# RWKV-7 and FFN step on one core: the end of the RWKV stage issued step by step between the first products of the first FFN

## The chip, the cores and the metric

One NeuronCore of a Trainium2 chip runs the whole kernel in one launch. The metric is the time of one execution on the device in microseconds (us). TensorE (PE) multiplies, VectorE (DVE) and ScalarE (ACT) do the elementwise work and empty PSUM, GpSimd (POOL) does a small share, and SyncE (SP) issues most of the DMA transfers; some are issued from ACT.

## The reference

The kernel computes one inference step of a two-layer decoder on 1024 prompt tokens and 64 sample tokens (8 requests of 8 tokens), 1088 tokens of width 1024 in all. Layer 0 mixes by a conformer convolution (512 channels) and by RWKV-7 (512 channels, 8 heads of 64); layer 1 mixes by pooling. After each mixing there is a SwiGLU FFN with a hidden width of 2816, and after each of the four sublayers a layer norm of the residual sum:

```
proj = x @ w_in
a_out, c_new = conformer_conv(proj[..., :1024], conv_prev, ...)
b_out, sh_new, s_new = rwkv_mix(proj[..., 1024:], shift_prev, wkv_prev, ...)   # o gets group norm, a bonus and a gate
mix = concat([a_out, b_out]) @ w_out
x = layer_norm(ALPHA * x + mix)
x = layer_norm(ALPHA * x + (silu(x @ wg) * (x @ wu)) @ wd)
```

rwkv_mix runs a recurrence over the tokens with one 64 x 64 state per head; the prompt is one sequence, the sample requests are eight short ones with states of their own.

## The kernel before

Tokens are cut into nine tiles: tiles 0 to 7 are 128 prompt tokens each, tile 8 the 64 sample tokens. Names in the program carry the tile's number; the trace leaves it out (`wo`, `xt`, `xo`, `bt_t`).

**Stages.** The in-projection, the convolution and the preparation of the recurrence (chunks, inverses of small triangular blocks on POOL) take the first part. A boundary follows in which the convolution halves of the out-projection (`wo<-hl_woA,ahl`) run while POOL inverts the last blocks. Then come eight RWKV loops (`chain`), one for each prompt tile, about 25 us each. Beside loop i the program issues filler work from a queue (`fq`): the preparation of the next tile, the group norm of the last (`gn_out`, tiles `gst_t`, `gmv_t`, `on_t`, then the transposes `pgn_t`, the gate `pg_t` and the gated output `bt_t`), the RWKV half of the out-projection of an older tile (`tail`, which is `wout`: 24 matmuls `wo<-hl_woB,bhl`, where `bhl` is `bt_t` split into two parts), and the transposes of a finished tile into the layout that the FFN reads (`xt`: 8 transposes of `y`, the scaling on ACT into `xo`, the store to `xtd` in DRAM).

**The end of the RWKV stage.** Behind loop 7 stand the sample unit (`chain_sample`: for each of four head pairs p the steps s0, products `sar` of the old state with mask `sm` and reduction `rS` on DVE; s1 and s2, products `spc`; s3, products `spo` and `sps` with mask `suv` and sums `Osb` and `ss`), the projections of tiles 6, 7 and 8, and the transposes of tiles 5 and 6. Only then the pools of the stage are closed and those of the FFN opened.

**FFN, first layer.** `early_x` loads the transposed activations of tokens 0 to 543 (`xe`, 4 loads of 544 KB) and splits them into the operands b11 and b21 (`b`). Stage 1a makes, for 11 pairs of blocks and for gate and up, one product of the upper left block of weights in two halves, which this text calls P1 (with b11) and P2 (with b21): 24 matmuls each, 44 halves in all. Two PSUM buffers of one tag hold a product (one for each 272 tokens), the tags taken in turn from `("mm", "o", "ch")`. After P1 ACT copies it out (`c`), after P2 ACT applies Silu (gate, `sg<-pa_g`) or DVE multiplies (up, `sg<-sg,pa_u`). P2 of a product stands behind P1 of the next. Weights are loaded (`raw_e`, 512 KB for a product) and split into `op_a` on ACT and DVE. `tick` issues one step of a second queue (`side`) about every 2 us of products: the transposes of tiles 7 and 8, then `late_x`, which loads all activations again (`xl`) and makes the operands t1 to t4 and b22 for stage 1b. Stage 1b begins with four sums of weight blocks on DVE (`s`, L1151) and their splits.

**Order.** On PE the order is the program's from loop 0 on. On the other engines a scheduler sets it at build time. PSUM has four tags (mm, o, ch, tp) of two buffers each.

The lines the change touches are in `phase2`, `chain_sample`, `gn_out`, `load_unit`, `early_x`, `load_w1`, `stage1a` and `build`.

Of the kernel before, what the change touches and what calls it, by code (L numbers as in the profile page):

```python
# [61 lines left out]
class Prog:  # L62
# [77 lines left out]
    def xt(self, l, i, y, pool, tag):  # L140
# [5 lines left out]
        def step(q):  # L146
            if q == 0:
                nc.scalar.dma_start(out=self.yd[l][i][:n], in_=y[:n])
# [36 lines left out]
    CAUTO = 8  # L185
# [7 lines left out]
    def consts(self, es, e1):  # L193
        tc, nc, I = self.tc, self.nc, self.I
        pool = lambda name, bufs=1, **kw: es.enter_context(tc.tile_pool(name=name, bufs=bufs, **kw))
        self.pp = pool("psum", 2, space=PSUM)
# [8 lines left out]
        self.c1d = [[self.dr.tile([128, TH], F32, name=f"c1d{l}_{x}") for x in range(NF)] for l in range(2)]  # L205
        self.hd = [[self.dr.tile([128, TOK], F32, name=f"hd{l}_{f}") for f in range(NF)] for l in range(2)]
# [12 lines left out]
    def phase1(self):  # L219
# [13 lines left out]
        pool = lambda name, bufs=1, **kw: es.enter_context(tc.tile_pool(name=name, bufs=bufs, side="right", **kw))  # L233
# [157 lines left out]
    def conv_a(self, i):  # L391
# [44 lines left out]
    def wout(self, i, get, w, alpha, after=None):  # L436
# [26 lines left out]
    def convs(self, wA):  # L463

        slots = []
        for x in range(11):
# [3 lines left out]
            if x >= 2:  # L470
                out += self.wout(x - 2, lambda j=x - 2: self.chl.pop(j), wA, ALPHA)
# [3 lines left out]
        return slots  # L475

# [191 lines left out]
    def load_unit(self, i):  # L668

        nc, up = self.nc, self.up  # L670
        u = type("Unit", (), {})()
        u.i, u.samp, u.nm = i, i == 8, f"t{i}"
# [7 lines left out]
        u.TT = up.tile([128, G, 64], F32, tag="TT", name=f"TT_{nm}")  # L680
# [8 lines left out]
        u.A21 = up.tile([128, G, 32], F32, tag="A21", name=f"A21_{nm}")  # L689
        u.ATm = [up.tile([128, G, 128], F32, tag=f"ATm{hd}", name=f"ATm{hd}_{nm}") for hd in range(2)]  # L690
# [5 lines left out]
        u.AR = up.tile([128, G, 2, 64], F32, tag="AR", name=f"AR_{nm}")  # L696
        u.BK = up.tile([128, G, 2, 64], F32, tag="BKh", name=f"BKh_{nm}")
        for t, d in ((u.AR, self.ard), (u.BK, self.bkd)):
            nc.sync.dma_start(out=t.rearrange("q (p c) s l -> q p (c s l)", p=4), in_=d[:, :, cs].rearrange("p q c s l -> q p (c s l)"))
        v = up.tile([128, 4, n], F32, tag="v", name=f"v_{nm}")  # L700
        u.bv = up.tile([128, 4, n], F32, tag="bv", name=f"bv_{nm}")
# [851 lines left out]
```

## Time and profile before

| | us |
|---|---|
| median of 3 runs (lowest, highest) | 2352.29 (2350.52, 2353.86) |
| the profiled execution | 2353.67 |
| its span | 2351.9 |
| PE busy | 2191.6 (93%) |
| DVE busy | 1558.9 (66%) |
| ACT busy | 910.3 (39%) |
| POOL busy | 449.3 (19%) |

The profile is one execution of the program with its instructions in time. Times in it count from the span's start. The profiled execution lies 1.38 us over the median. The granted clock (PEclk) is TensorE's clock as a share of full speed, averaged over a stretch.

### The profile page before, as it was taken

To read this page: it belongs to the slowest core of one execution; us is meant where nothing else is said; L and a number is where in the kernel's file an instruction comes from. 1 tells how busy PE (TensorE), PEld (TensorE's weight loads), DVE (VectorE), ACT (ScalarE), POOL (GpSimd) and SP (SyncE) were. 2 spreads that over 40 slices of the span, in tenths; PEclk is the share of its full clock that TensorE was granted. 3 is DMA by queue.
4 is the path that set the end of the run, shared out by engine and by line. 5 is a ranking of instruction groups with operands and counts; after the bars stand their busy time and mean duration, and the time that the engine had idled before them with its cause. 6 is when DMAs were issued, how large, how long until landed. Compare 5 with 4: busy or idle time off the path is not lost.

```text
span 2351.9 us, 39322 instructions
## 1 busy us (share of the span) xinstructions
PE 2191.6 (93%) x15026; PEld 1971.6 (84%) x15026; DVE 1558.9 (66%) x2859; ACT 910.3 (39%) x2041; POOL 449.3 (19%) x551
## 2 busy tenths in 40 slices
PE   8898898869896899999999999989999999999998
PEld 7887787657664799999997787879999999977886
DVE  6987698734457535777767657455477777667565
ACT  3243244445642543333333434343443333334332
POOL 3588866563111000000000101000000000000010
PEclk9999899679998999999999999999999999999999
DMA  5132326745532654333348555444463333376662
GB/s 169 48 116 75 108 86 193 230 124 152 158 95 98 228 193 148 113 119 120 120 128 268 186 163 185 141 157 159 159 222 120 120 120 120 121 241 188 218 199 92
DMA packets 234362, 352.83 MB, mean 150 GB/s; under 512 B 73461, under 2 KB 151597, under 8 KB 234164
## 3 DMA queue, kind: packets, MB, share of 16 engines
q1 hardware_dynamic: 187294, 284.01, 39.1%
q10 hardware_dynamic: 46878, 66.30, 8.0%
q8 instruction: 118, 1.93, 0.3%
q14 instruction: 72, 0.59, 0.1%
HBM read 261.72 MB, written 88.74 MB: 149 GB/s over the span
## 4 chain that ended last, share of the span: by engine, by line
PE 60%; DVE 4%; DMA 4%; issue 2%; ACT 1%; SPq 0%; POOL 0%; ACTq 0%; POOLq 0%; DVEq 0%
PE dn L75 17%; DMA yr<-yd 1%; PE wo L75 1%; PE pp L75 1%; PE pl L75 1%; DMA b<-lnv 1%; PE pa_1u L75 1%; DVE op_d L96 1%; PE pa_10u L75 1%; PE pa_4g L75 1%; PE pa_2g L75 1%; PE pa_5g L75 1%; PE pa_3u L75 1%; PE pa_2u L75 1%; PE pa_3g L75 1%
## 5 line engine op out<-in xcount | busy, mean ns | idle before, releaser
L75 PE MATMUL dn<-op_d,h 128*128 128x512 f32 (+1 forms) x2288 | 544.7, 395 | 16.7 <-ACT op_d L72 6.6
L75 PEld LDWEIGHTS dn<-op_d,h 128*128 128x128 f32 (+1 forms) x2288 | 422.1, 187 | 117.9 <-DVE op_d L96 8.4
L75 PE MATMUL in<-xh,hl_in 128*128 128x384 f32 (+1 forms) x1056 | 282.5, 348 | 15.8 <-ACT xh L72 7.5
L104 POOL TENSOR_TENSOR rstd_f<-rs_f,mhalf 128x1 f32<-128x1 f32 (+1 forms) x18 | 36.3, 2017 | 1328.2 <-DVE rs_f L103 762.4
L96 DVE TENSOR_TENSOR op_d<-raw_d,op_d 128x512 fp32r<-128x512 f32 x264 | 179.2, 685 | 161.5 <-ACT op_d L72 161.0
L72 ACT ACTIVATE op_d<-raw_d 128x512 fp32r<-128x512 f32 x264 | 163.4, 625 | 292.4 <-PE dn L75 262.2
L75 PEld LDWEIGHTS in<-xh,hl_in 128*128 128x128 f32 x1056 | 199.0, 200 | 28.4 <-ACT xm L345 8.0
L312 DVE SCALAR_TENSOR_TENSOR acc<-u,hv,acc 128x1024 f32<-128x1024 f32 x120 | 193.2, 1619 | 0.8
L75 PE MATMUL in<-xl,hl_in 128*128 128x384 f32 (+1 forms) x528 | 182.7, 346 | 2.2 <-DVE xl L96 2.2
L75 PEld LDWEIGHTS in<-xl,hl_in 128*128 128x128 f32 x528 | 105.7, 200 | 5.4 <-DVE xl L96 2.9
L96 DVE TENSOR_TENSOR h<-hr,h 128x384 fp32r<-128x384 f32 (+2 forms) x176 | 72.8, 433 | 15.4 <-ACT h L72 15.4
L72 ACT ACTIVATE h<-hr 128x384 fp32r<-128x384 f32 (+2 forms) x176 | 69.2, 416 | 17.1 <-DMA hr<-hd 12.5
L156 ACT ACTIVATE xo<-xt,vec 128x128 f32<-128x128 f32 (+1 forms) x144 | 53.0, 452 | 44.1 <-PE xt L154 43.1
L75 PE MATMUL wo<-hl_woB,bhl 128*128 128x512 f32 (+1 forms) x216 | 65.0, 445 | 5.0 <-ACT bhl L72 4.9
L104 POOL TENSOR_TENSOR rstd_m<-rs_m,mhalf 128x1 f32<-128x1 f32 (+1 forms) x18 | 11.3, 629 | 271.2 <-DVE rs_m L103 264.7
L91 POOL TENSOR_TENSOR hl_in<-raw_in,hl_in 128x1024 fp32r<-128x1024 f32 x21 | 58.5, 2785 | 15.7 <-ACT hl_in L72 15.7
L75 PE MATMUL wo<-hl_woA,ahl 128*128 128x512 f32 (+1 forms) x216 | 57.6, 418 | 0.8 <-DVE y L456 0.4
L75 PEld LDWEIGHTS wo<-hl_woB,bhl 128*128 128x128 f32 (+1 forms) x216 | 41.2, 202 | 18.5 <-ACT bhl L72 6.0
L75 PEld LDWEIGHTS wo<-hl_woA,ahl 128*128 128x128 f32 (+1 forms) x216 | 40.6, 194 | 11.1 <-DVE y L456 0.7
L72 ACT ACTIVATE rw<-in 128x384 f32<-128x384 f32 (+2 forms) x56 | 22.0, 394 | 46.1 <-PE in L75 30.9
L75 PE MATMUL pl<-hl_pw,phl 128*128 128x256 f32 (+1 forms) x216 | 33.4, 286 | 3.3 <-DVE phl L96 2.8
L320 POOL TENSOR_TENSOR prod<-u,hv 128x496 f32<-128x496 f32 x16 | 30.6, 1915 | 29.9 <-DVE u L293 16.3
(1040 smaller groups left out, 4769.8 us busy)
## 6 DMA issues: line engine op xcount, KB each, us to landing
raw_d<-ffn_down SPq DMA_DIRECT2D x132, 512.0 KB, 3.8
hd<-sg ACTq DMA_DIRECT2D x88, 272.0 KB, 4.1
hr<-hd SPq DMA_DIRECT2D x88, 192.0 KB, 3.7
raw_in<-w_in SPq DMA_DIRECT2D x22, 512.0 KB, 4.3
xl<-xtd SPq DMA_DIRECT2D x16, 544.0 KB, 4.6
ATm_t<-atd SPq DMA_DIRECT2D x16, 512.0 KB, 5.3
yr<-yd SPq DMA_DIRECT2D x16, 512.0 KB, 5.7
xtd<-xo ACTq DMA_DIRECT2D x28, 256.0 KB, 3.7
```

The costliest lines, as they stand in the source:

```text
L72: self.nc.scalar.activation(out=out, in_=in_, func=AF.Copy)
L75: self.nc.tensor.matmul(out, lhsT, rhs, start=start, stop=stop, **kw)
L91: (eng or nc.gpsimd).tensor_tensor(out=hl[:, 1, :], in0=raw, in1=hl[:, 0, :].bitcast(F32), op=ALU.subtract)
L96: (eng or self.nc.vector).tensor_tensor(out=out_lo, in0=src, in1=out_hi.bitcast(F32), op=ALU.subtract)
L104: nc.gpsimd.tensor_tensor(out=out, in0=t[:P, :n], in1=self.mhalf[:P, :n], op=ALU.pow)
L156: nc.scalar.activation(out=xo[:, k, :n], in_=ps[:, k * 128:k * 128 + n], func=AF.Identity, scale=self.v("lng", 16 * l + 4 * q + k), bias=s ...
L312: nc.vector.scalar_tensor_tensor(out=out, in0=src, scalar=cw(j), in1=out, op0=ALU.mult, op1=ALU.add)
L320: nc.gpsimd.tensor_tensor(out=prod, in0=win, in1=taps, op=ALU.mult)
```

## The change

- The end of the RWKV stage no longer stands ahead of the FFN as one piece. Loop 7 is followed by the sample unit's s0 of all pairs, the projection and group norm steps of tiles 6 and 7 that can run, s1 and s2 (now merged over the four pairs into one PSUM buffer, `spc`) and the transposes of tile 5. Then stage 1a begins, one pair of blocks at a time, and the projection of tile 7, s3 of the four pairs, the sample's group norm, the transposes of tiles 6 and 7, the projection of tile 8 and its transposes are steps of `side` between its products. They end with the fourth pair of blocks; the other seven pairs run with `late_x` as before.
- Less is resident: four buffers for `y` in place of nine (after the convolution half of the out-projection y is stored to DRAM as `yad` and loaded again as `yb` for the other half), the gated output is stored (`btd`) and loaded again (`bl`) for its projection, two `bt` buffers, and pools that wait by tile. `early_x` loads b11 and b21 apart in 8 loads of 272 KB through the two `wraw` buffers, which then also take the weights of stage 1a of the first layer (before: 5 buffers). That stage has 4 operand buffers in place of 7 and takes its PSUM tags from `("o", "ch")`, since the steps between use `mm` and `tp`. In the program as built, the first sum of stage 1b (`s1_0_0g`) and the splits behind it lie in SBUF over operand buffers of stage 1a, the sum over that of its last product.
- Layer 1 loads `early_x` in 8 loads too; the rest of it is as before.

The core of the diff (renamed pools, tags and DRAM tiles left out):

```diff
-    def early_x(self, l):
+    def early_x(self, l, names=("b11", "b21")):
...
-            xf = self.rawp.tile([128, 2, TH], F32, tag="rw", name=f"xe{l}_{k}")
-            self.nc.sync.dma_start(out=xf, in_=self.xtd[l][0][:, k::4, :])
+                xf = self.raw_w(f"xe{l}_{k}{n}")[:, :TH]
+                self.nc.sync.dma_start(out=xf, in_=self.xtd[l][0][:, k + 4 * (n == "b21"), :])
...
+    def raw_w(self, name):
+        if self.rawp is None:
+            return self.wraw.tile([128, 1024], F32, tag="raw", name=name)
...
-            pa = [self.psum(tags[n % 3], f"pa{nm}{s}") for s in range(2)]
+            pa = [self.psum(tags[n % len(tags)], f"pa{nm}{s}") for s in range(2)]
...
+    def load_y(self, i):
+        n = TT_TILES[i][1]
+        self.y[i] = self.ypool.tile([128, D], F32, tag="y", name=f"yb{i}")
+        self.nc.sync.dma_start(out=self.y[i][:n], in_=self.yad[i][:n])
+        self.bt[i] = self.bp.tile([128, 4, n], F32, tag="bt", name=f"bl{i}")
+        self.nc.sync.dma_start(out=self.bt[i], in_=self.btd[i][:, :, :n])
...
+        S0, S12, S3, out = self.chain_sample(us[8])
+        self.load_y(6)
+        before()
+        self.fill(2.5)
+        t6, t7 = tail(6), tail(7)
+        self.PG = "tp"
+        self.fq.extend(S0[:1] + t6[:2] + [(1.4, lambda: gn[7]())])
+        self.fill(1e9)
+        self.load_y(7)
+        e7.close()
+        between()
+        self.fq.extend(S0[1:3] + t6[2:3] + S0[3:] + t6[3:] + S12 + xt(5))
+        self.fill(1e9)
...
+        self.side.extend(only(t7[:1] + S3[:2] + t7[1:2] + S3[2:] + t7[2:]) + [gn8] + only(xt(6))
+                         + [lambda: (ge["f"](), self.load_y(8))] + only(xt(7)) + [lambda: None] * 2 + only(t8)
+                         + [lambda: None] * 2 + only(xt(8)))
...
+                def before():
+                    self.xap = pool("xa01", es=ea)
+                    for f in self.early_x(0, ("b11",)):
+                        f()
+
+                def between():
+                    self.hlp = pool("ops0", 4, es=ea)
+                    self.tmp1 = pool("tmp0", es=ea)
+                    self.xap = pool("xa02", es=ea)
+                    for f in self.early_x(0, ("b21",)):
+                        f()
+                e3 = self.phase2(before, between)
+                self.PA, self.SG, self.C1 = ("o", "ch"), 2, 2
+                self.sg, self.nA, p = {}, 0, 0
+                while self.side:
+                    self.stage1a(0, [p])
+                    p += 1
...
+                    self.side.extend(self.late_x(0, xb))
+                    self.stage1a(0, range(p, NF // 2))
```

Three places of the order, in which numbers in names are buffers; `0_4g` is layer 0, block pair 4, gate.

PE at the start of stage 1a, before: the last projection (tile 8, `wo_35`, `wo_36`) ends right ahead of the first product.

```order
L154 MATMUL xt_6_0_7573<-ident,y_4072 128x128 x4
L154 MATMUL xt_6_1_7584<-ident,y_4072 128x128 x4
L75 MATMUL wo_35_7594<-hl_woB_5562,bhl_7596 64x512
L75 MATMUL wo_36_7595<-hl_woB_5562,bhl_7596 64x512
...
L75 MATMUL pa_0g_7696<-b_0_7668,op_a_0_0g 128x272
```

The same place with the change (`wo_33`, `wo_34` are tile 7, `sps` is s3):

```order
L75 MATMUL spc<-sw,TT_t_6940 64x64 x8
L155 MATMUL xt_5_0_7502<-ident,yb_6965 128x128 x4
L155 MATMUL xt_5_1_7513<-ident,yb_6965 128x128 x4
L75 MATMUL pa_0g_7525<-b_0_7243,op_a_0_0g 128x272
...
L75 MATMUL wo_33_7548<-hl_woB_5597,bhl_7550 128x512
...
L75 MATMUL spo<-SUV_t_6964,ATm_t_6947 64x64
```

The projections of tiles 7 and 8, s3 and the transposes of tile 6 moved behind the first product; s1 and s2, and so all of s0, still stand ahead of it.

DVE at the end of stage 1a, before (`s_0_0g` are the sums of stage 1b's first product, `sg_7` to `sg_10` the multiplications that empty the last up products):

```order
L1104 TENSOR_TENSOR sg_7_0_8844<-sg_7_0_8844,pa_7u_8785 128x272
L96 TENSOR_TENSOR op_a_0_10g<-raw_e_10g,op_a_0_10g 128x512
L1151 TENSOR_TENSOR s_0_0g<-raw_b_0g 128x512
L1151 TENSOR_TENSOR s_0_0g<-s_0_0g,raw_a_0g 128x512
...
L96 TENSOR_TENSOR op_s_0_0g<-s_0_0g,op_s_0_0g 128x512
...
L1104 TENSOR_TENSOR sg_10_0_9234<-sg_10_0_9234,pa_10u_9174 128x272
```

With the change:

```order
L1135 TENSOR_TENSOR sg_9_0_9167<-sg_9_0_9167,pa_9u_9108 128x272
L1135 TENSOR_TENSOR sg_10_0_9297<-sg_10_0_9297,pa_10u_9237 128x272
L1135 TENSOR_TENSOR sg_10_0_9297<-sg_10_0_9297,pa_10u_9238 128x272
L1182 TENSOR_TENSOR s_0_0g<-raw_b_0g 128x512
L1182 TENSOR_TENSOR s_0_0g<-s_0_0g,raw_a_0g 128x512
L1182 TENSOR_TENSOR s_0_0g<-raw_a_0g,raw_b_0g 128x512
L1182 TENSOR_TENSOR s_0_0g<-raw_a_0g,s_0_0g 128x512
L96 TENSOR_TENSOR op_s_0_0g<-s_0_0g,op_s_0_0g 128x512 x3
```

The sums and the first split moved behind the multiplication that waits for the last product of stage 1a.

DVE ahead of the first product, with the change, from the gated output of tile 7 on (`sm`, `rS` are s0; `b` is b21 from `xe`; `op_a_0_0g` the first product's weights; before, this work stood apart, the splits of `xe` behind all of it):

```order
L893 TENSOR_TENSOR bt_t_7364<-bt_t_7364,pg_t_7363 128x512
L914 TENSOR_TENSOR sm_7411<-sar_7409,c_smask 128x512
L96 TENSOR_TENSOR b_0_7390<-xe_0b_7391,b_0_7390 128x544
L96 TENSOR_TENSOR b_0_7390<-xe_1b_7395,b_0_7390 128x544
L916 TENSOR_REDUCE rS_7413<-sm_7411 128x64
...
L96 TENSOR_TENSOR op_a_0_0g<-raw_e_0g,op_a_0_0g 128x512
L914 TENSOR_TENSOR sm_7449<-sar_7447,c_smask 128x512
L916 TENSOR_REDUCE rS_7451<-sm_7449 128x64
...
L916 TENSOR_REDUCE rS_7458<-sm_7456 128x64
```

All eight masks and reductions of s0 now share DVE's queue, in this order, with the splits that the first product needs.

## Rows read from the trace of the kernel before

**Rows 1.** The page: busy time by engine, and the granted clock in 40 equal slices

```profile
PE 2191.6 (93%) x15026; PEld 1971.6 (84%) x15026; DVE 1558.9 (66%) x2859; ACT 910.3 (39%) x2041; POOL 449.3 (19%) x551
...
PEclk9999899679998999999999999999999999999999
```

**Rows 2.** Windows: span, busy us (and instructions) by engine, granted clock, DMA share

```profile
505.00:705.00 200.00, 180.93 (x2297) 137.66 (x2297) 95.27 (x304) 109.15 (x279) 53.06 (x79) 0.92 0.47 129
705.00:768.60 63.60, 41.33 (x208) 24.36 (x206) 45.05 (x120) 18.26 (x49) 9.46 (x9) 0.82 0.33 113
768.60:803.00 34.40, 28.11 (x186) 26.46 (x187) 13.25 (x22) 17.86 (x42) 0.00 (x0) 0.89 0.57 185
803.00:914.00 111.00, 111.00 (x889) 111.00 (x888) 56.67 (x94) 48.83 (x111) 0.00 (x0) 1.00 0.61 208
```

**Rows 3.** PE's waits, 705 to 803: what waited, for what, us in total, times, longest

```profile
PE pa_0g L75 <- ACT op_a_0g L72: 10.5, 1, 10.5
PE wo L75 <- ACT bhl L72: 4.9, 2, 2.7
PE sar L75 <- DVE sm L896: 3.4, 1, 3.4
PE pa_0u L75 <- ACT op_a_0u L72: 2.5, 1, 2.5
```

**Rows 4.** Timeline: SP's queue ahead of the FFN; columns start, us, engine, instruction, [idle before]

```profile
736.48 23.58 SPq L1051 DMA_DIRECT2D xe<-xtd  x4
762.55 0.66 ACT L72 ACTIVATE b<-xe 128x544 fp32r<-128x544 f32 x1 [9.80 <-DMA xe<-xtd]
```

**Rows 5.** Timeline of PE in the sample unit, and the transposes of a tile

```profile
726.73 1.65 PE L75 MATMUL wo<-hl_woB,bhl 128*128 128x512 f32 x6
728.31 0.45 PE L75 MATMUL spo<-SUV_t,ATm_t 128*64 128x64 f32 x4
728.59 1.23 PE L75 MATMUL sps<-suv,BKT_t 128*64 128x512 f32 x4
741.86 1.03 PE L154 MATMUL xt<-ident,y 128*128 128x128 f32 x8
```

**Rows 6.** Timeline of DVE behind loop 7, and the splits of xe

```profile
710.84 2.10 DVE L860 TENSOR_SCALAR on_t<-po_t,gmv_t,grs_t 128x64 f32<-128x64 f32 x8 [1.51 <-POOL grs_t L104]
712.87 1.27 DVE L896 TENSOR_TENSOR sm<-sar,c_smask 128x512 f32<-128x512 f32 x2
714.06 1.95 DVE L898 TENSOR_REDUCE rS<-sm 128x64 f32<-128x512 f32 x2
715.92 0.69 DVE L896 TENSOR_TENSOR sm<-sar,c_smask 128x512 f32<-128x512 f32 x1
762.24 3.89 DVE L96 TENSOR_TENSOR b<-xe,b 128x544 fp32r<-128x544 f32 x6
```

**Rows 7.** Timeline of stage 1a in its steady part: how its products are emptied

```profile
863.05 0.69 ACT L1101 ACTIVATE sg<-pa_6g 128x272 f32<-128x272 f32 x2 [1.80 <-PE pa_6g L75]
869.07 0.78 DVE L1104 TENSOR_TENSOR sg<-sg,pa_6u 128x272 f32<-128x272 f32 x2 [1.08 <-PE pa_6u L75]
```

**Rows 8.** Timeline from stage 1a to stage 1b

```profile
883.54 0.69 DVE L1151 TENSOR_TENSOR s_0g<-raw_b_0g 128x512 f32<-128x512 f32 x1 [0.97 <-DMA raw_b_0g<-ffn_gate]
885.48 0.68 DVE L1151 TENSOR_TENSOR s_0g<-raw_a_0g,s_0g 128x512 f32<-128x512 f32 x1
914.10 3.17 PE L75 MATMUL pb_0g<-t,op_s_0g 128*128 128x272 f32 x24
```

**Rows 9.** Timeline of the boundary ahead of loop 0

```profile
462.60 0.24 POOL L662 TENSOR_TENSOR xt<-X,At 128x31 f32<-128x31 f32 x1 [3.27 <-DMA X<-xinitP]
469.62 0.54 POOL L104 TENSOR_TENSOR crs<-rs_c,mhalf 128x1 f32<-128x1 f32 x1
504.53 1.09 PE L749 MATMUL pT_t<-ident,TT_t 128*128 128x128 f32 x4 [9.95 <-POOL xt_None L662]
```

**Rows 10.** Transfers 690 to 790: count, KB each, median us to landing

```profile
xe<-xtd SPq DMA_DIRECT2D x4, 544.0 KB, 4.3
```

More of the change, by code (lines that the diff above doesn't have):

```diff
@@ L138, in load_gb, with xt @@
         return g, b
[L140 removed]
+    def xt(self, l, i, pool, tag):
         nc = self.nc
@@ L205, in consts @@
         self.c1d = [[self.dr.tile([128, TH], F32, name=f"c1d{l}_{x}") for x in range(NF)] for l in range(2)]
+        self.yad = [self.dr.tile([128, D], F32, name=f"yad{i}") for i in range(9)]
+        self.btd = [self.dr.tile([128, 4, 128], F32, name=f"btd{i}") for i in range(9)]
         self.hd = [[self.dr.tile([128, TOK], F32, name=f"hd{l}_{f}") for f in range(NF)] for l in range(2)]
@@ L678, in load_unit @@
         cs = slice(c0, c0 + nch)
-        u.TT = up.tile([128, G, 64], F32, tag="TT", name=f"TT_{nm}")
+        u.TT = up.tile([128, G, 64], F32, tag="TT" + tag, **kw, name=f"TT_{nm}")
         nc.gpsimd.memset(u.TT, 0.0)
@@ L688, in load_unit @@
             nc.sync.dma_start(out=u.TT[r0:r0 + 32, :, b * 32:b * 32 + 32], in_=src)
-        u.A21 = up.tile([128, G, 32], F32, tag="A21", name=f"A21_{nm}")
-        u.ATm = [up.tile([128, G, 128], F32, tag=f"ATm{hd}", name=f"ATm{hd}_{nm}") for hd in range(2)]
+        u.A21 = up.tile([128, G, 32], F32, tag="A21" + tag, **kw, name=f"A21_{nm}")
+        u.ATm = [up.tile([128, G, 128], F32, tag=f"ATm{hd}" + tag, **kw, name=f"ATm{hd}_{nm}") for hd in range(2)]
         for hd in range(2):
@@ L757, in two @@
             pX = self.psum("tp", f"pX_{nm}")
-            t.X1 = up.tile([128, G, 32], F32, tag="X1", name=f"X1_{nm}", bufs=1)
+            t.X1 = up.tile([128, G, 32], F32, tag="X1" + u.tag, name=f"X1_{nm}", bufs=1)
             for g in range(G):
@@ L930, in s3, with phase2 @@
             nc.sync.dma_start(out=O["new_wkv_s"][:, p], in_=s1_)
-        return s0, s1, s2, s3, [Osb[:, hd].rearrange("p c v -> p (c v)") for hd in range(2)]
-    def phase2(self):
+        S = lambda f, c: [(c, lambda p=p: f(p)) for p in range(4)]
+        return S(s0, 1.1), [(0.4, s1), (0.4, s2)], S(s3, 1.3), [Osb[:, hd].rearrange("p c v -> p (c v)") for hd in range(2)]
+    def phase2(self, before, between):
         tc, nc, I, O = self.tc, self.nc, self.I, self.O
         es = ExitStack()
-        pool = lambda name, bufs=1, **kw: es.enter_context(tc.tile_pool(name=name, bufs=bufs, side="right", **kw))
+        pool = lambda name, bufs=1: self.pool(es, name, bufs, side="right")
         cp = pool("rconst")
@@ L981, in mix @@
             return out
-        for x in first[:self.CAUTO]:
+        for x in slots[:8]:
             self.fq.extend(x)
@@ new lines, in phase2 @@
+        S0, S12, S3, out = self.chain_sample(us[8])
[10 more added lines that the diff above has]
+        self.fq.extend(S0[1:3] + t6[2:3] + S0[3:] + t6[3:] + S12 + xt(5))
+        self.fill(1e9)
+        only = lambda steps: [f for _, f in steps]
+        ge = {}
@@ L1072, in step @@
             if x == 0:
-                t["x"] = [self.rawp.tile([128, 2, TH], F32, tag="rw", name=f"xl{l}_{k}{j}") for j in range(2)]
+                t["x"] = [(self.rawp or self.rawl).tile([128, 2, TH], F32, tag="rw", name=f"xl{l}_{k}{j}") for j in range(2)]
                 for j in range(2):
```

215 lines of the change are left out of this document (108 added, 107 removed).

## The prediction, made before the changed kernel was run

> **What bounds the kernel now.** I read the page first: PE is busy for 93% of the span, so time is to be won only where it isn't, and the row of the granted clock has its low digits in two places, ahead of and behind the RWKV loops [rows 1]. The table of windows prices the second place [rows 2]: from 705 to 768.6 PE is busy for 41.3 of 63.6 us at a clock of 0.82, from 768.6 to 803 for 28.1 of 34.4 at 0.89, and from there to 914 without a gap at 1.00. Idle time is thus 22.3 + 6.3 = 28.6 us, and no reordering of this stretch wins more than that and its slow clock. The waits say what it is made of: 10.5 us in one wait of the first FFN product for its weights, 3.4 for a mask of the sample unit, 4.9 for splits of gated outputs, 2.5 for the next weights [rows 3]. The timeline shows why the longest exists: SP's load of the FFN's input `xe` stands in its queue from 736.48 for 23.58 us (its buffers lie where the last projection still reads), and ACT's first split behind it starts at 762.55, after 9.8 us without work [rows 4]. So the end of the stage is bound first by DVE (45 busy us of 63.6, most of it ahead of 740), then by that load.
>
> From here I count against the profiled execution: the sum is a difference, and it is added to the median of 2352.3, as that execution lay 1.4 us above it.
>
> **1. The FFN starts earlier.** Before the first product stand, with the change, only s0 to s2 of the sample, the projection of tile 6 and the transposes of tile 5; the load waits for nothing of tiles 7 and 8. DVE then decides. Behind loop 7 its `on_t` runs from 710.84 to 712.87 [rows 6]; what leaves loop 7 (two s0 steps) and what enters it (the first splits of b11) I let cancel. From there its queue, in the new order, holds eight masks at 0.60 from start to start (712.87, 714.06: two in 1.19), eight reductions at 0.93 (714.06, 715.92) and four splits of b21 at 0.65 (six in 3.89) [rows 6]; eight smaller or like steps (two of `bt`, one of `bhl`, four of the first weights, one sum of y) I take at 0.6: 4.8 + 7.4 + 2.6 + 4.8 = 19.6. That is 732.5; s1, s2 and the transposes of tile 5 take some 2 and 1.03 [rows 5]: 735.5. The inputs now come through two buffers in turn, at up to 4.3 us a transfer of 544 KB [rows 10]; I add 3.5 for what of this isn't hidden. The first product starts at 739 instead of 768.6: **-29.6**. Bounds: 734 if nothing waits and loop 7 ends earlier; 745 if four transfers, each 4.3 and two splits of 0.65, follow each other from 712.9 with the weights' last (735.3) and all later DVE work behind them.
>
> **2. What had stood ahead of it now stands between the products.** Six matmuls of a projection take 1.58 (726.73 to 728.31), 24 so 6.3, for tiles 7 and 8 together 12.6; s3 of one pair runs from 728.31 to 729.82, four 6.0; the transposes of tile 6 take 1.03, and the sample's group norm about as much [rows 5]. **+20.6.** Their DVE and ACT work stands beside products: in full run DVE is busy for 57 of 111 us and ACT for 49 [rows 2], and a step comes each 2 us. The transposes of tiles 7 and 8 were between products before.
>
> **3. The FFN's slow start.** 186 matmuls from 768.6 to 803 took 34.4 us; at 111.00 / 889 = 0.125 us they take 23.3, so 11.1 were lost to weights that came late and a clock of 0.89 [rows 2]. With PE kept at work, and the order P1, P1, P2, P2 of the first four pairs, in which each product has 3 us to be emptied, I take 8 of it as gone: **-8**, between -11 and -3 (the weights now have two buffers).
>
> **4. Two PSUM tags instead of three.** From the fifth pair on, P1 of a product needs the buffers of the one before the last right behind its P2. Both halves must be emptied first, as the second matmul writes the second half. ACT starts 0.07 after the end and takes 0.69 for both; DVE takes 0.78 [rows 7]. With three tags this costs nothing (111.00 us busy of 111 [rows 2]); with two PE waits for 0.8 to 0.9 at every change from a product to the next but one, 12 times from pairs 4 to 10: **+10.2**. Below 5 it can't well come, since nothing lies between; above, to 18, if a split of 0.65 stands ahead each time.
>
> Whether the clock stays full over these gaps is open. The loops, with 19 of 200 us idle, were granted 0.92 [rows 2]; I take 1.00, as gaps of 0.85 in 6.9 us are shorter than most of theirs. The Trainium skill has a rule that speaks against it: "TensorE: Matmul & The Clock Gate", section "A second HAM failure mode: psum-queue depth-cycling", says that a kernel that cycles through PSUM banks, with PE idling briefly and often between groups, loses speed because its clock falls and rises again. No row here shows such a stretch; it is a rival below.
>
> **5. From stage 1a to 1b.** Before, the sums for stage 1b ran at 883.54 to 886.2, and its first product followed at 914.10 with no gap [rows 8]. Now the first sum is written over an operand of stage 1a's last product, so it waits for that. After the end come the multiplication, 0.78 [rows 7], four sums (1.94 to the start of the last, and 0.68 [rows 8]) and the split on DVE (0.69 by its like); ACT's part runs beside, and four matmuls need that alone: **+3.7**, between 2.9 and 4.4.
>
> **6. Elsewhere.** At the boundary, POOL's inversion of the last blocks runs from 462.60; a small step of the convolution (`crs`) comes in its midst, at 469.62, and PE's first transposes for loop 0 wait for POOL until 504.53, 9.95 us of it idle [rows 9]. In the new order that `crs` stands ahead of the inversion, which thus waits for it: **+3**, between 0 and 8 (469.62 - 462.60, and a step more). In the loops a projection now waits for a store and a load of its input, a loop ahead of its use: **+1**, 0 to 3. About 45 more transfers on SP are spread over 250 us in which the DMA engines are busy for less than half [rows 2]; they cost nothing unless one is waited for in order.
>
> Sum: -29.6 + 20.6 - 8 + 10.2 + 3.7 + 3 + 1 = **+0.9**, 2353.2; I say 2353. The idle time is filled, and what is given for the room (a PSUM tag, early sums, POOL's order) costs nearly as much. 0.2% is 4.7 us, about what a measurement of this kernel can tell from no change.
>
> **Rivals.**
> *A, the fill wins.* The FFN starts at 735, its slow start is gone (-11), and boundary and loops cost nothing: -33.6 + 20.6 - 11 + 10.2 + 3.7 = -10.1, 2342. For it: `xe` had waited for buffers, not for bandwidth [rows 4]. Against: the two-buffer round trips.
> *B, PSUM waits behind splits.* In pairs 4 to 10 `late_x` puts its splits in ACT's and DVE's queues; if one stands ahead of the Silu or multiplication each time, 12 x 0.65 = 7.8 is added: 2361. It decides from about half of the changes on (+3.9, 2357). For it: two queues that run in order, one of which waits for loads of `xl`. Against: in the trace of before the emptying starts 0.07 behind the product, with the same splits in the queue [rows 7].
> *C, the clock falls in the two-tag stretch* to the loops' 0.92 [rows 2]: its 24 product halves of 3.0 us take 72 x (1/0.92 - 1) = 6.3 more: 2359. That is the way the skill's rule would act here.
> *D, the change doesn't do what it says:* the FFN's inputs come so late through two buffers that it starts at 755 or later: +16, 2369.
>
> **How the numbers follow.** Forecast 0.35, A 0.32, B 0.18, C 0.07, D 0.08. The range runs from 2340 (A, its price a little overshot) to 2367, short of D: 0.15 to 0.2 are left out. The chances are A for faster, 0.32, the forecast's own case for within 0.2%, 0.35, and B, C and D for slower, 0.33.
>
> **What would show it.** The first `pa_0g` of the new trace between 734 and 745 in before's time (less what the boundary added); waits of some 0.8 us of `pa` for `sg`, 12 of them, at a clock of 1.00; a gap of 3 to 4 us at the first `pb_0g`; `pT_t` of loop 0 later than 504.5. I am wrong if the products of pairs 4 to 10 follow without gaps, if those gaps exceed 1.5 us each, or if the loops themselves have become longer by more than 3 us.

## The result, and the profile after

| | us |
|---|---|
| changed kernel, median of 4 runs (lowest, highest) | 2370.18 (2365.17, 2372.58) |
| kernel before, the 3 runs shown above and one more on the same chip | 2351.4 (2346.61, 2353.86) |
| ratio, with its 95% interval | 1.008 (1.0056 to 1.0104) |
| profiled execution, its span | 2365.17, 2362.7 |

The change made the kernel slower by 0.8%, 19 us in the medians; 2353 was forecast, and the upper end of the range was 2367. The profiled execution is the shortest of the four. Three profiles of each kernel were taken in the end (the later ones are told of below), so that stretches can be compared by their means.

The page of the changed kernel, answering to [rows 1]; busy time has hardly moved:

```profile
PE 2202.2 (93%) x15026; PEld 1979.1 (84%) x15026; DVE 1559.8 (66%) x2856; ACT 912.1 (39%) x2035; POOL 445.7 (19%) x551
...
PEclk9988899679988999999999999999999999999999
```

The windows of the changed kernel, answering to [rows 2]: from loop 7 to the first product, the first four pairs of blocks, and the other seven in three pieces.

```profile
705.00:747.80 42.80, 33.09 (x199) 20.21 (x199) 34.72 (x73) 13.99 (x34) 6.90 (x7) 0.75 0.43 129
747.80:818.00 70.20, 70.20 (x502) 62.59 (x500) 35.22 (x85) 28.44 (x72) 2.92 (x4) 0.99 0.50 161
818.00:840.00 22.00, 18.30 (x136) 17.65 (x135) 14.39 (x25) 12.47 (x27) 0.00 (x0) 0.97 0.79 267
840.00:880.00 40.00, 35.02 (x246) 33.49 (x246) 21.64 (x36) 17.64 (x38) 0.00 (x0) 0.93 0.43 143
880.00:922.00 42.00, 39.22 (x297) 37.44 (x295) 8.23 (x15) 11.53 (x27) 0.00 (x0) 1.00 0.53 179
```

The columns are those of [rows 2]. The second row is what the change was to bring: no idle time on PE for 70.2 us, where before 6.3 of the first 34.4 us behind `pa_0g` were idle [rows 2]; the wait of 10.5 ahead of that product [rows 3] is gone as well. The last three rows are where before all 111 us were busy; now 104 us hold 92.5 of work. PE's waits in the changed kernel, 747.5 to 930 (the longest twelve), say for what:

```profile
PE pb_0g L75 <- ACT op_s_0g L72: 2.8, 1, 2.8
PE pa_7g L75 <- ACT sg L1132: 2.8, 1, 2.8
PE pa_5g L75 <- ACT sg L1132: 1.9, 1, 1.9
PE pa_5u L75 <- DVE sg L1135: 1.8, 1, 1.8
PE pa_8u L75 <- DVE sg L1135: 1.1, 1, 1.1
PE pa_6u L75 <- DVE sg L1135: 0.8, 1, 0.8
PE pa_6g L75 <- ACT sg L1132: 0.7, 1, 0.7
PE pa_9u L75 <- DVE sg L1135: 0.6, 1, 0.6
PE pa_7u L75 <- DVE sg L1135: 0.4, 1, 0.4
PE pa_10u L75 <- DVE sg L1135: 0.4, 1, 0.4
PE pb_0g L75 <- DVE op_s_0g L96: 0.4, 1, 0.4
PE pa_8g L75 <- ACT sg L1132: 0.4, 1, 0.4
```

There are twelve waits of a product for a Silu or a multiplication, one for each change of product, as forecast; but from 5g to 8u they reach from 0.4 to 2.8, and only from 9g on are they all short, 0.4 to 0.6. The timelines show what the long ones are made of: ACT and DVE ahead of `sg` of pair 4, ACT ahead of that of pair 6 with the load that it waits for, and PE behind them.

```profile
827.35 0.66 ACT L72 ACTIVATE b<-xl 128x544 fp32r<-128x544 f32 x1 [2.43 <-DMA xl<-xtd]
828.18 0.66 ACT L72 ACTIVATE t<-t1f 128x544 fp32r<-128x544 f32 x1 [0.17 <-DVE t1f L1094]
828.75 0.67 ACT L1132 ACTIVATE sg<-pa_4g 128x272 f32<-128x272 f32 x2
...
836.90 0.78 DVE L1135 TENSOR_TENSOR sg<-sg,pa_4u 128x272 f32<-128x272 f32 x2
...
855.94 0.69 DVE L96 TENSOR_TENSOR op_a_6u<-raw_e_6u,op_a_6u 128x512 fp32r<-128x512 f32 x1
856.66 0.33 SPq L1122 DMA_DIRECT2D raw_e_7u<-ffn_up  x1
861.51 0.63 ACT L72 ACTIVATE op_a_7u<-raw_e_7u 128x512 fp32r<-128x512 f32 x1 [4.07 <-DMA raw_e_7u<-ffn_up]
862.05 0.67 ACT L1132 ACTIVATE sg<-pa_6g 128x272 f32<-128x272 f32 x2
...
829.18 3.45 PE L75 MATMUL pa_5g<-b,op_a_5g 128*128 128x272 f32 x24 [1.85 <-ACT sg L1132]
...
837.48 4.94 PE L75 MATMUL pa_5u<-b,op_a_5u 128*128 128x272 f32 x24 [1.84 <-DVE sg L1135]
...
862.48 4.84 PE L75 MATMUL pa_7g<-b,op_a_7g 128*128 128x272 f32 x24 [2.75 <-ACT sg L1132]
```

`b<-xl` and `t<-t1f` are splits of `late_x`; they stand ahead of the Silu of 4g, one of them after waiting for its load. On DVE 15 steps run without a gap from 827.42 to 836.90 ahead of the multiplication of 4u, 13 of them `late_x`'s. The Silu of 6g stands behind a weight split that waits 4.07 us for its load. SP had issued that load only at 856.66, when DVE had split `op_a_6u` and so freed one of the two weight buffers; the split of `op_a_6u`, at 855.94, stood among the last steps of `late_x` on DVE. The products behind the gaps of 1.84 and 2.75 us took 4.94 and 4.84 us, where those behind 0.4 took 3.5; the one behind the gap of 1.85 at 5g took 3.45.

At the boundary, first the load of the inversion's input X on SP before, which [rows 9] don't show, then the changed kernel, answering to [rows 9] (SP's queue, POOL, PE):

```profile
458.08 0.36 SPq L657 DMA_DIRECT2D X<-xinitP  x1
```

```profile
463.87 1.24 SPq L674 DMA_DIRECT2D X<-xinitP  x1
...
468.14 1.30 POOL L835 TENSOR_TENSOR sw_t<-SUV_t,WC_t 64x256 f32<-64x256 f32 x2 [5.67 <-DMA WC_t<-wcd]
469.52 0.24 POOL L679 TENSOR_TENSOR xt<-X,At 128x31 f32<-128x31 f32 x1
...
511.60 1.09 PE L767 MATMUL pT_t<-ident,TT_t 128*128 128x128 f32 x4 [14.28 <-DMA TT_t<-dxp]
```

The inversion begins 6.92 us later and loop 0 starts 7.07 us later. The load of X was issued at 458.08 before and is issued at 463.87 now, as five loads of unit 0 stand ahead of it on SP. On POOL `sw_t`, which had waited for one of these loads, ends 0.08 us before the inversion begins.

All stretches, as means of three profiles of each kernel (the first product halves of pair 4 mark the seams; one half product of 3.0 us that stood behind the first `pa_4g` now stands ahead of it and is put back):

| stretch | before | changed | difference | forecast |
|---|---|---|---|---|
| start to first `pT_t` | 504.5 | 510.9 | +6.4 | +3 |
| loops, first to last `pT_t` | 180.2 | 185.0 | +4.8 | +1 |
| last `pT_t` to first `pa_0g` | 81.7 | 53.4 | -28.3 | -29.6 |
| to first `pa_4g`, less the half product | 58.9 | 67.3 | +8.4 | +12.6 |
| to first `pc_0g`, with it | 90.2 | 114.1 | +23.9 | +13.9 |
| to the end | 1434.7 | 1434.6 | -0.1 | 0 |
| span | 2350.2 | 2365.3 | +15.1 | +0.9 |

### The profile page after: what moved, and what is told of

It is laid out like the page before. It is cut to its first block, busy times and chain, and to the rows that moved or that the text cites. A ratio compares the mean times of both kernels' runs of the same rounds, so it can differ in the third digit from the quotient of the medians.

```text
span 2362.7 us, 39379 instructions
## 1 busy us (share of the span) xinstructions
PE 2202.2 (93%) x15026; PEld 1979.1 (84%) x15026; DVE 1559.8 (66%) x2856; ACT 912.1 (39%) x2035; POOL 445.7 (19%) x551
## 4 chain that ended last, share of the span: by engine, by line
PE 65%; DVE 15%; POOL 6%; DMA 6%; issue 5%; ACT 2%; SPq 1%; POOLq 0%; DVEq 0%; ACTq 0%
PE dn L75 18%; DVE acc L317 5%; PE wo L75 2%; PE in L75 2%; PE pp L75 1%; POOL xt L679 1%; POOL X L681 1%; PE po_t L75 1%; PE pl L75 1%; DMA xl<-xtd 1%; PE pc_t L75 1%; DVE xt L679 1%; PE xt L155 1%; DMA raw_d<-ffn_down 1%; DVE yr L1263 1%
## 5 line engine op out<-in xcount | busy, mean ns | idle before, releaser
L96 DVE TENSOR_TENSOR op_d<-raw_d,op_d 128x512 fp32r<-128x512 f32 x264 | 179.4, 686 | 162.6 <-ACT op_d L72 162.2
L96 DVE TENSOR_TENSOR h<-hr,h 128x384 fp32r<-128x384 f32 (+2 forms) x176 | 72.9, 433 | 10.2 <-ACT h L72 10.2
```

The source lines that it names most:

```text
L96: (eng or self.nc.vector).tensor_tensor(out=out_lo, in0=src, in1=out_hi.bitcast(F32), op=ALU.subtract)
```

## The experiments

Medians stand beside runs of the kernel before on the same chip: 2352.61 (20 runs) for the first four, 2353.61 (11) for the next four, 2352.53 (23) for the ninth to eleventh, 2353.18 (17) for the rest. Where ten or more executions of a kernel were timed, they spread over 10 to 21 us, so the stretches in the trace decide more than a median does.

**Three tags again, from the fifth pair on.**

```diff
+                    self.PA = ("ch", "o", "mm")
                     self.stage1a(0, range(p, NF // 2))
```

> The changed kernel with the third PSUM tag back from the fifth pair of blocks of the first stage 1a on (the steps that needed it are done by then); nothing else changed. Theory (PSUM): the 19.8 us that pairs 4 to 10 lost against 28 product halves of 3.007 us are waits of a product for the emptying of the one before the last, 12 at 0.8 to 0.9 us, and about 9.6 more where Silu or multiplication stood behind the splits of late_x; with three tags each emptying has a product's 3 us, so the stretch from the first pa_4g to the first pb_0g shrinks from 107 to 88 to 91 us and the kernel by 16 to 19. Rival (late inputs): the long gaps come from transfers (two weight buffers, the loads of xl) that would hold PE with any tags: the four long gaps stay, some 10 us, and the kernel gains 8 to 10.

Median 2356.39, ratio to before 1.0025 (1.0005 to 1.0045). From `pa_4g` to `pb_0g` 92.85 us, where the changed kernel took 106.98: 14.1 won; 88 to 91 had been expected. No wait for `sg` is left; the longest are for weights, 1.3 for `op_a_6u`. Of the 19.5 us that the changed kernel's first profile lost up to the first `pa_10u` 5.7 are left. So the two tags carry the forecast 10.2 and part of what came on top: `late_x` stands in the queues of ACT and DVE at the same time as with the change, but with a third tag no product waits for an emptying behind it.

**Two tags, one pair at a time.**

```diff
-                    self.stage1a(0, range(p, NF // 2))
+                    for q in range(p, NF // 2):
+                        self.stage1a(0, [q])
```

> The changed kernel with two tags as it is, but pairs 4 to 10 of the first stage 1a issued one pair at a time (P1 gate, P1 up, P2 gate, P2 up), as the first four are. Theory (PSUM): not the count of tags costs but that a product follows right behind the emptying of its own buffers; in this order each emptying has 3 us, the 12 waits go and the kernel gains 16 to 19 us, as with three tags. Rival (late inputs): gains 8 to 10 at most. A third view, that PSUM traffic of any kind slows products here: no gain.

Median 2348.94, ratio 0.999 (0.9975 to 1.0005). `pa_4g` to `pb_0g` 90.0 us, 17.0 less than with the change, and at two tags. PE's waits in that stretch, all of them:

```profile
PE pb_0g L75 <- ACT op_s_0g L72: 2.8, 1, 2.8
PE pa_5u L75 <- ACT c_5u L72: 0.6, 1, 0.6
PE pa_5u L75 <- DVE sg L1135: 0.5, 1, 0.5
PE pb_0g L75 <- DVE op_s_0g L96: 0.4, 1, 0.4
PE pa_6u L75 <- DVE sg L1135: 0.3, 1, 0.3
```

In the order P1g, P1u, P2g, P2u a tag has a whole product half, 3.0 us, between its last use and its next. A third tag gives that distance too; it is the distance that decides, and two tags are enough for it.

**The sums' pool opened first.**

```diff
-            self.hlp = pool("ops", 7)
             self.stp = pool("sums", 4)
+            self.hlp = pool("ops", 7)
```

> The changed kernel with the pool of stage 1b's sums placed ahead of its operand buffers, so that the first sums no longer lie over the operand of stage 1a's last product. Theory (memory): the 3.7 us between the last product of stage 1a and the second of stage 1b come from that overlap; the sums now run before the end, the gap shrinks to at most 1.6 us (a multiplication and a split may still stand in line) and the kernel gains 2 to 4 us. Rival (weights): stage 1b's weights land late because their buffers are those of stage 1a; the gap stays above 3 us and the time as it is.

The sums ran at 917.97 to 920.65, ahead of the end of the last product, and the gap shrank:

```profile
920.81 3.17 PE L75 MATMUL pa_10u<-b,op_a_10u 128*128 128x272 f32 x24
923.81 0.66 PE L75 MATMUL pb_0g<-t,op_s_0g 128*128 128x272 f32 x4
925.39 2.78 PE L75 MATMUL pb_0g<-t,op_s_0g 128*128 128x272 f32 x20 [0.91 <-DVE op_s_0g L96]
928.00 2.18 PE L75 MATMUL pc_0g<-t,op_s_0g 128*128 128x272 f32 x16
```

From `pa_10u` to `pc_0g` are 7.19 us; two halves take 6.01, so 1.18 is lost, and 3.72 was with the change. The median, 2365.99, ratio 1.0059 (1.0037 to 1.0082), can't show 2.5 us.

**The last inversion, first try.** Loop 0's zero state by a memset, and the sample's inversion moved from POOL to DVE.

```diff
-    PINV = (0, 3, None)
+    PINV = (0, 3)
...
+            if u.i == 0 and c == 0:
+                nc.vector.memset(sw, 0.0)
-            for hd in range(2):
+            for hd in range(2 if u.i or c else 0):
```

> The changed kernel with two things taken from POOL's queue ahead of loop 0: the product of loop 0's zero state with its decay (written as zeros by DVE, same value; it had waited for a load), and the inversion of the sample's blocks, which runs on DVE. Theory (POOL's order): loop 0 begins 7.1 us late because the last inversion began at 469.5 instead of 462.6, behind that product; it now begins at about 466, runs alone at 0.9 to 1.0 us a step, and the first pT_t comes at 501 to 505 instead of 511.6: the kernel gains 6 to 10 us. Rival (transfers): the wait at pT_t is named as one for a load, and the 45 more transfers delay that load by themselves; pT_t stays above 509 and the kernel gains less than 3.

Missed: median 2377.17, ratio 1.0107 (1.008 to 1.0135). With POOL free the inversion began at 477.03 and `pT_t` came at 517.45. In the new order SP issues the load of X at 471.98, behind all loads of units 0 and 1. The profile puts the end of POOL's wait down to a store that SP issued just ahead of that load, at 470.48. So without `sw` on POOL the inversion is held by SP's queue, and longer than before.

**Without late_x.**

```diff
+        if l == 0:
+            for n in ("t1", "t2", "t4", "t3", "b22"):
+                X[n] = pool.tile([128, 2, 4, TH], F32R, tag=n, name=f"{n}_{l}")
+                nc.gpsimd.memset(X[n].bitcast(F32), 0.0)
+            return []
         return [lambda k=k, x=x: step(k, x) for k in range(4) for x in range(6)]
```

> late_x of layer 0 is left out (its five operands are set to zero by POOL ahead of their use), everything else is the changed kernel: two PSUM tags, the same order of products. Theory (the extra 9.6 us over 12 x 0.85 came from late_x's splits standing ahead of the Silu and the multiplication in ACT's and DVE's queues, and from the clock after the gaps so made): from the first pa_4g to the first pb_0g 84.2 + 10.2 + 3.7 = 98 us where the changed kernel took 107, each change from a product to the next but one loses 0.8 to 1.2, the products behind them run at the full clock, and the median is 2361. Rival (the two tags alone cost it, with the clock falling over many short gaps): the stretch stays at 104 or more, with granted clock below 0.97 in it, and the median at 2367 or more.

From `pa_4g` (827.53) to `pb_0g` (925.54) 98.01 us: the theory said 98, the rival 104. Windows of this kernel, and two of its twelve waits:

```profile
827.50:842.50 15.00, 14.60 (x115) 14.26 (x114) 3.00 (x5) 6.11 (x16) 11.28 (x4) 1.00 0.48 160
842.50:872.50 30.00, 27.67 (x205) 25.90 (x204) 8.50 (x16) 10.20 (x22) 3.49 (x1) 1.00 0.41 132
872.50:922.50 50.00, 47.59 (x359) 45.43 (x358) 10.07 (x18) 14.03 (x33) 0.00 (x0) 1.00 0.49 171
```

```profile
892.48 3.43 PE L75 MATMUL pa_9g<-b,op_a_9g 128*128 128x272 f32 x24 [0.36 <-ACT sg L1137]
...
899.39 3.50 PE L75 MATMUL pa_9u<-b,op_a_9u 128*128 128x272 f32 x24 [0.48 <-DVE sg L1140]
```

From `pa_4g` to the first `pa_10u`, 25 halves of 3.007 later, 10.4 us are lost, 0.87 a change: the wait of 0.4 for the first half of the buffer, and a slower start behind it, as the second matmul waits for the other half. With `late_x` it is 19.3 (19.5, 18.6, 19.9 in three profiles). Its work in the queues, with its loads, thus costs 8.9, the clock behind the long gaps included. The median, 2366.19 (2361 was expected), hides it: this profile's loops took 190.4 us and its first four pairs of blocks 74.1, where the changed kernel's first profile has 183.4 and 70.3.

**The inversion's input on POOL's queue.** The two edits of the first try, and:

```diff
-            nc.sync.dma_start(out=At[x * nb:x * nb + nb], in_=src)
+            (nc.gpsimd if p == 3 else nc.sync).dma_start(out=At[x * nb:x * nb + nb], in_=src)
...
-        nc.sync.dma_start(out=X[:P, :R], in_=self.I["xinitP" if p is not None else "xinitS"][:P])
+        (nc.gpsimd if p == 3 else nc.sync).dma_start(out=X[:P, :R], in_=self.I["xinitP" if p is not None else "xinitS"][:P])
```

> Three edits to the changed kernel, all at the boundary: the zero state of loop 0 is a memset, the sample's inversion runs on DVE, and the two inputs of the last inversion (At and X) are loaded from POOL's own queue rather than SP's. Theory (SP's order of that load decides when the inversion starts): it starts at 464 to 465, right behind the crs at 462 and the landing of X, instead of 469.5; runs alone in 31.5 us; first pT_t at 503 to 505 instead of 511.6; the median 6 to 8 lower than the changed kernel, 2363. Rival (POOL's or DVE's queue decides, or the splits of the loops suffer from the sample's inversion on DVE): pT_t at 509 or later, or loops longer by what was won, and a median of 2368 or more.

Missed by far: median 2389.02, ratio 1.0149 (1.0126 to 1.0171).

```profile
466.37 0.59 POOL L674 DMA_DIRECT2D X<-xinitP  x1 [8.67 <-DMA dxp<-X]
473.06 0.23 POOL L679 TENSOR_TENSOR xt<-X,At 128x31 f32<-128x31 f32 x1 [6.10 <-DMA X<-xinitP]
...
483.64 0.56 POOL L104 TENSOR_TENSOR crs<-rs_c,mhalf 128x1 f32<-128x1 f32 x1 [7.91 <-DVE rs_c L103]
```

X has one buffer, and the load waits for the store of the inversion before (`dxp<-X`), which now stands later on SP. The inversion thus began 3.5 us later than with the change, but `pT_t` came 10.4 later, at 522.0: in the midst of the inversion `crs` waits 7.91 us for DVE, and the store of its result stood 3.0 us behind its end on SP. **All three repairs together** met the same:

> The three repairs together: one pair of blocks at a time in all 11 pairs, the pool of the sums opened ahead of that of the operands, and the boundary's edits (memset, sample inversion on DVE, inversion inputs loaded from POOL's queue). If the three causes are separate they add up: 2370 - 17 (pa_4g to pb_0g at 90 or less) - 2.5 (gap at pb_0g about 1.2) - 7 (pT_t about 504) = 2343, 0.4% below the kernel before. If one of them only moves a wait to a later place, it stays at 2347 or more.

Median 2364.81 (2343 if they add up), ratio 1.0059 (1.0037 to 1.0081): `pT_t` at 520.5 ate much of what the FFN gave (`pa_4g` to `pb_0g` 87.2).

**The changed kernel again.**

> The changed kernel, unchanged, for a second profile and more times. Theory (the stretches around the boundary and from pa_4g to pb_0g repeat; only the loops vary from one execution to another, with the clock granted in them): pT_t at 511 to 513, pa_4g to pb_0g at 105 to 109 with the same long waits (pa_5g, pa_5u, pa_7g), loops (first to last pT_t) anywhere from 183 to 191, median 2366 to 2372. Rival (the long waits are chance): the long waits fall at other products or are gone, and the stretch differs by more than 4.

Median 2367.18, ratio 1.0063 (1.0045 to 1.0081). `pT_t` at 511.0, `pa_4g` to `pb_0g` 106.05, and the same long waits (7g 2.7, 5u 1.8, 5g 1.7; 6g had 1.4 here). The loops took 190.3.

**The FFN's two repairs, and five loads moved to ACT's queue.** The ninth kernel has the pair order and the sums' pool first. The tenth has also, for v and bv as shown, and for AR, BKh and WC alike:

```diff
-            nc.sync.dma_start(out=t, in_=d[:, :, t0:t0 + n].rearrange("p q t -> q p t"))
+            (nc.scalar if i < 1 else nc.sync).dma_start(out=t, in_=d[:, :, t0:t0 + n].rearrange("p q t -> q p t"))
```

> The two repairs inside the FFN together, the boundary left as the change has it: one pair of blocks at a time in all 11 pairs, and the pool of the sums opened ahead of that of the operands. If they are separate: from the first pa_4g to the first pb_0g 87 to 89 us (107 in the changed kernel, 90.0 with the pair order alone), a gap of 1.2 at pb_0g, and the median 2349 - 2.5 = 2346.5, against 2353 of the kernel before; ratio 0.997. If the sums' gain is hidden by something else, the median stays at 2349 and the ratio at 0.999.

> The same two repairs, and at the boundary five loads of unit 0 (AR, BKh, v, bv, WC) are issued from ACT's queue instead of SP's, so that on SP the load of X for the last inversion stands ahead of unit 1's loads and right behind At. Theory (SP's queue ahead of X sets when the inversion starts): X is issued by 461.5 instead of 463.9 and the inversion starts 2 to 4 us earlier than 469.5, pT_t of loop 0 at 507 to 510 instead of 511.6, and the median 2 to 4 below that of the two repairs alone. Rival (the store of the inversion before, from the same buffer, or the wait of sw for WC sets it): no earlier than 468.5, the median as with the two repairs.

The two repairs: median 2348.92, ratio 0.998 (0.9966 to 0.9994), `pa_4g` to `pb_0g` 87.22 as expected, the median no better than with the pair order alone. With the loads on ACT: median 2356.98, ratio 1.0021 (1.0004 to 1.0038). X was issued at 463.56, where the ninth kernel has 463.45: ACT's copy into `ATm_p3b`, at 452.47 there, came at 458.59, behind the loads in its own queue and eight steps of the convolution, and the store of the inversion before moved from 453.97 to 457.31 on SP. The inversion itself began at 469.15, 0.9 us earlier than in the ninth kernel, but took 39.4 us instead of 34.8, as 54 steps of the sample's inversion stood between its own on POOL, where 33 had; so `pT_t` came at 515.9 instead of 512.1. None of the three edits to the boundary won its 6 us back.

**The kernel before again, and sw on DVE.** In loop 3 of the changed kernel `sw_t` stands ahead of `grs_t` on POOL, and PE waits 1.95 us for `on_t` where it had waited 0.17. Was it this that made the clock fall in the loops? The twelfth and thirteenth kernels are the ninth with

```diff
-                nc.gpsimd.tensor_tensor(out=sw[H[hd]], in0=SUV[H[hd], c, 0, hd], ...
+                nc.vector.tensor_tensor(out=sw[H[hd]], in0=SUV[H[hd], c, 0, hd], ...
```

> The kernel before, unchanged, for a second profile. Theory (the loops vary from one execution to the next in both kernels, with the clock granted): first to last pT_t anywhere from 182 to 191 (182.4 in its first profile; 183 to 191 in the five of the changed kernels), and the boundary (pT_t at 504.5) and stage 1a (145.5 from the first pa_0g to the first pb_0g) as in the first. Rival (the change made the loops longer): 182 to 184 again, so that 5 us of the 18 belong to the loops.

> The two FFN repairs (one pair at a time, sums' pool first) and one edit in the loops: sw_t (state times decay) is computed on DVE instead of POOL, so that in loop 3 grs_t no longer stands behind it on POOL. Theory (POOL's order in loop 3 opens a gap of 1.9 us on PE, behind which the clock falls in most executions): the wait of pgn_t for on_t in loop 3 is back to 0.2 to 0.4, no half-clock stretch begins 64 to 84 us behind the first pT_t, first to last pT_t 178 to 184, and the median 3 to 6 below the two repairs alone (2348.9), 2344. At the boundary the inversion no longer waits for sw either, up to 1.1 us. Rival (the loops' clock varies by chance, or DVE's 16 further steps delay the recurrence): first to last pT_t 185 to 192, the median at 2348 or more.

> The same kernel for a second profile. Theory: again no half-clock stretch 64 to 84 us behind the first pT_t, and first to last pT_t 178 to 184. Rival: anywhere in 183 to 192.

> The changed kernel for a third profile. Theory: the wait of 1.9 us in loop 3 again, a half-clock stretch beginning 64 to 84 us behind the first pT_t in it or not (it was there in five of seven profiles), first to last pT_t 183 to 191. Rival (chance): below 182.

> The kernel before for a third profile. Theory: no half-clock stretch beginning 64 to 84 us behind the first pT_t, first to last pT_t 178 to 184. Rival (chance): 185 or more.

Windows of the loops (first to last `pT_t`; the third-last number is the granted clock), first the kernel before in its third profile, then the changed kernel in its third, then in its second, then `sw` on DVE twice:

```profile
504.80:684.00 179.20, 162.22 (x2129) 125.25 (x2130) 83.00 (x279) 98.92 (x249) 52.12 (x78) 0.93 0.51 139
```

```profile
510.20:691.50 181.30, 162.14 (x2129) 124.50 (x2130) 84.69 (x284) 99.20 (x249) 48.38 (x65) 0.94 0.63 183
```

```profile
511.00:701.30 190.30, 171.01 (x2129) 131.92 (x2130) 83.40 (x277) 99.35 (x249) 46.65 (x62) 0.88 0.60 173
```

```profile
510.60:695.40 184.80, 166.52 (x2130) 127.71 (x2130) 96.69 (x307) 99.36 (x249) 29.51 (x36) 0.91 0.62 178
```

```profile
510.40:691.70 181.30, 162.32 (x2129) 124.78 (x2130) 95.99 (x306) 99.16 (x249) 29.09 (x35) 0.94 0.63 183
```

The theory fell. The changed kernel's third profile has the gap in loop 3 (2.05 us) and a clock of 0.94; with `sw` on DVE that gap was gone in the twelfth run and the clock was 0.50 from 580 to 588 all the same. Median 2349.08, ratio 0.9977 (0.9959 to 0.9996), no better than the ninth kernel. The kernel before took 182.4, 179.1 and 179.2, the changed one 183.4, 190.3 and 181.3. In the changed kernel loops and clock go together: 181.3 at 0.94, 190.3 at 0.88, with PE idle for 19.2 and 19.3 us in the two. Against the kernel before the clock is not all: its third profile has PE busy for 162.2 us, as the changed kernel's third has, and idle for 17.0. The eleventh run was expected at 182 to 191 and came at 179.1, the fourteenth at 183 to 191 and came at 181.3, the rival's place; both forecasts missed. The five kernels of the first three and of the fifth and ninth experiments have their edits behind the loops in the program; their loops took 191.3, 184.0, 188.3, 190.4 and 187.3, so that of eight profiles of these loops seven are longer than all three of before.

## Why the prediction was wrong

**1, the earlier start** (-29.6): measured -28.3. The count of DVE's queue ahead of the first product held in the main: the last reduction of s0 ended 22.8 us behind `on_t`, not 19.6, and the first product came 4.1 behind that; the 3.5 set aside for late inputs covered most of the difference.

**2 and 3, the moved work and the slow start** (+20.6 - 8): measured +8.4. The slow start is gone in full (-11.1, not -8), so the moved work cost about 19.5 by what is left; PE was busy for 70.20 of 70.20 us.

**4, two tags** (+10.2, upper bound 18): this is the step that failed; measured 19.3. It took the emptying to start right behind the product, and that holds only where nothing else is in the queues. There its price is right: 10.4 without `late_x`, with a wait of 0.4 to 0.7 at each. Rival B named what was added, 7.8 by its price, and 8.9 came. That the two are close is in part luck: B counted a split of 0.65 at each of twelve changes, and what came are four waits of 1.1 to 2.8 us, one of them for a weight load, and a lower clock behind some of them. Against B the prediction had put that in [rows 7] the emptying starts 0.07 behind its product "with the same splits in the queue". That reading was false. The rows are from 863 and 869; in that trace the last split of `late_x` on ACT is this:

```profile
828.27 0.67 ACT L72 ACTIVATE t<-t3f 128x544 fp32r<-128x544 f32 x1
```

On DVE its last split began at 829.59; `late_x` had thus ended 33 us before the rows shown. With the change it stands behind the end of the RWKV stage in `side`, and so its splits begin at 827, in the very stretch that has two tags: the words "as before" in the section on the change hold for what `late_x` does, not for when. The scheduler placed its steps ahead of the Silus and multiplications there.

Of the 8.9, the clock is a part: in the first profile the two products behind gaps of 1.84 and 2.75 us took 4.94 and 4.84 us instead of 3.5, together 2.8. Behind the same two gaps the second profile has 4.93 and 3.45, the third 4.93 and 5.87, so 1.5 and about 4. Rival C, a clock of 0.92 over the whole stretch, did not come: without `late_x` twelve gaps of 0.4 to 0.7 us in 86 us left it at 1.00, and with it the stretch from `pa_4g` to `pb_0g` was granted 0.97, 0.98 and 0.95. The rule of the Trainium skill ("TensorE: Matmul & The Clock Gate", section "A second HAM failure mode: psum-queue depth-cycling"), that the clock goes down and up where PE idles briefly and often between groups, would have it fall in such a stretch; the trace does not agree for gaps this short. The prediction had taken 1.00 because gaps of 0.85 were shorter than most of those in the loops. That was misread: of the 37 gaps that make up the 19 us before, five are longer. So 1.00 was right, where the gaps stayed short, for a reason that doesn't hold.

**5, from stage 1a to 1b** (+3.7): 3.72 in the first profile; 4.6 as a mean with the slower start of `pa_10u` and, in the third, `pb_0g` at half clock (4.30 us for the 20 matmuls that took 2.78 in the first). The mechanism is shown by the sums' pool: 1.18 is left when the sums lie elsewhere. The terms that the prediction lists for it come to 4.1, and how 3.7 follows from them is not worked out there, so the close fit is in part luck.

**6, elsewhere** (+3, +1): the boundary cost 6.4, within its bounds of 0 to 8, but not by the mechanism named. `crs` ran at 461.94 and delayed nothing there (in the sixth kernel it did, for 7.91 us). In all seventeen traces the inversion begins 3.7 to 7.0 us behind the issue of the load of X (462.60 behind 458.08 before, 469.52 behind 463.87 with the change, 473.06 behind 466.37, 477.03 behind 471.98). So 5.8 of the 6.9 us are the later issue on SP. `sw` on POOL has a smaller part, up to about a microsecond: where the inversion begins right behind `sw`, as in the changed kernel, that is 5.6 to 6.8 us behind the issue, and in the four later kernels that load X from SP and have no `sw` right ahead of the inversion 5.0 to 5.6 (with `sw` on DVE 468.06 behind 462.83). I had read POOL's order where SP's was the one that mattered most. Moving that load ahead was tried and not achieved, so this account rests on the traces and on no repair. The loops cost 4.8 rather than 1, more than the 3 that the prediction named as a sign of being wrong: 1.8 in idle time of PE (18.0, 19.3 and 19.2 us where 17.2, 16.9 and 17.0 had been), the other 3.0 in its busy time, which goes with the clock. Seven of eight profiles above all three of before speak for the change and against chance, but the one cause that was tried fell, and the cause stays open. Without the loops the miss would have been 10 us.

Together: 9.1 (step 4), 3.4 (boundary), 3.8 (loops), 0.9 (step 5) and 1.3 (step 1) too little, 4.2 (steps 2, 3) too much: 14.3, the 15.1 us measured less the 0.9 forecast but for rounding. The medians put the difference at 19 and, for the changed kernel run again, at 13.6.

What the change won, the earlier start, is real. Two edits that touch none of its moves, the order of the products and of two pools, bring it to 2348.92, 0.2% below the kernel before and 18 to 21 us below itself (2367.18 and 2370.18).

## What to carry to other kernels

A row that shows a fast hand-over proves it only for what stood in the queues at that moment: ask when each filler runs before and after the change, and price a rotating buffer by what the emptying engine will have in its queue then. With few buffers, reorder the work so that something stands between a buffer's last use and its next; here that cost nothing and gave back 17 us. When a scheduler sets the order of a DMA queue, look for the load that the longest serial piece of work starts with.

## What the runs showed of the hardware that was not expected

- The same loops took 181.3 and 190.3 us in two profiles of one kernel, with PE idle for 19.2 and 19.3 us in them and a granted clock of 0.94 and 0.88. The execution with the shorter loops was yet the longer of the two, 2370.05 against 2367.57, by its other stretches.
- A gap on PE may or may not be followed by a lower clock: behind 1.84, 1.83 and 1.95 us at `pa_5u` the product took 4.93 to 4.94 us in all three profiles, behind 1.85, 1.72 and 1.62 at `pa_5g` 3.45 to 3.46, behind 2.75, 2.70 and 2.76 at `pa_7g` 4.84, 3.45 and 5.87.
- Freeing an engine can delay it: two edits that took work off POOL made the scheduler reorder SP, and POOL started 7.5 us later (469.52 to 477.03).
- Five loads put on ACT's queue moved a copy on ACT by 6.1 us (452.47 to 458.59) and won nothing on SP: the load of X was issued at 463.56 where it had been at 463.45.
